# A decoder trunk whose SBUF pools are shifted by small free pieces

## The chip, the cores and the metric

One core of a Trainium2 chip runs the whole program. The metric is the device time of one execution in microseconds. Before the change it is 1892.44 us, the median of three runs (1891.72 to 1893.65 us).

## The reference

Two decoder layers on 256 tokens of 1024 channels, all in float32. Each layer first mixes tokens (three branches fed by one projection), then applies a feed-forward part: a dense SwiGLU in the first layer, two of eight SwiGLU experts per token in the second.

```python
for l in range(DEPTH):
    h = rms_norm(x) * (1 + sc1) + sh1
    x = x + g1 * token_mixer(h, ...)   # gated delta net, Mamba-2, latent attention, gates, w_out
    h = rms_norm(x) * (1 + sc2) + sh2
    if l % 2 == 0:
        f = swiglu(h, ffn_w_gate[i], ffn_w_up[i], ffn_w_down[i])      # 1024 -> 2816 -> 1024
    else:
        f = moe_ffn(h, router, w_gate, w_up, w_down)                  # 8 experts, 1024 -> 3584 -> 1024
    x = x + g2 * f
return rms_norm(x, final_norm_w)
```

## The kernel before, in words

Every large product is made from two halves of each operand, high and low (float32r): `mm3` (line 98) issues three matmuls, high by high, high by low and low by high, through the helper `mm` (line 95, whose instruction stands at line 96). The first operand of `mm` is stationary, the second is streamed; the profile names a matmul as output<-streamed,stationary.

Weights come in pieces of 1 MB (128 partitions x 2048 columns) by DMAs on SyncE's queue into `raw` buffers of 8 KB per partition, requested ahead. `chunk` (line 160) splits a piece: ScalarE copies 1024 columns into a high half `whi` (line 170), VectorE subtracts it for the low half `wlo` (line 172). The halves lie in a ring (line 151): four buffers of 4 KB of each kind and, in the expert stage, for every fifth one more in another pool. TensorE's use of a buffer is what gives it back to ScalarE, and the low half's reading of a raw buffer is what lets the next load start.

The stages in order:

- `mixer` of layer 0 and 1 (line 533). Its projections stream either the weights with the activations `hh`/`hl` stationary (`tok_gemm`, `tmajor_gemms`), 512 columns wide, or, in `conv` (line 563), the activations with the weights stationary, 256 columns wide. Branch projections have `yh`/`yl` stationary. The output projection (`tmajor_gemms`, line 430, called at the end of `mixer`) takes its first column half out of the ring and its second out of 2 KB tiles `ohi`/`olo` in the mixer's own pool (`wg`, line 539).
- `dense_ffn` (line 1222) with `hh`/`hl`, then `ah`/`al` stationary.
- `moe` (line 1310): eight times `expert` (line 1551), each for up to 128 tokens that `gather` (line 1507) picked by a product with a selection matrix `Pm` into `xx`. Gate and up: seven groups of 512 hidden columns, in each 48 matmuls that stream the ring with `xx` stationary, then `inner` (line 1558: SiLU, product, four transposes, split into `act`). Down: 168 matmuls that stream the ring with `act` stationary. `outer` (line 1589) scales the result and adds it to the tokens by a product with `PTm`; it runs beside the next expert's first groups. The order of ScalarE's and VectorE's instructions around the splits is fixed by `behind`, which queues an instruction after a named one on its engine.

SBUF is laid out by pools, from the left end upward and, for pools with side="right", from the right end downward; within a pool tiles follow each other in the order of their first use, in steps of 32 bytes. Where the operands start, modulo 256 bytes, by the program's list of tiles:

| tiles | start in bytes | modulo 256 |
| --- | --- | --- |
| `raw`, `whi`, `wlo` (pool wp) | 35296, 59872, 76256 | 224 |
| `hh`, `hl` (and `h2` in their place later) | 92640, 100832 | 224 |
| `act`, `tg`, `ah`/`al`, `yh`/`yl` of the mixer, other tiles of the right side | right side ends at 229344 | 224 |
| the mixer's 2 KB tiles (`ohi`, `olo` and others) | from 113760 | 96 |
| `Pm` | 109312 | 0 |
| `xx`, `sg`, `PTm` of the experts | 117856, 134240, 140384 | 96 |
| `yh` of the experts' output | 142656 | 64 |
| `xs`, `cst` | 17024, 25216 | 128 |

Pieces inside a tile that a matmul reads begin at multiples of 512 bytes from the tile's start, but for the 336-column pieces of the small projection.

Of the kernel before, what the change touches and what calls it, by code (L numbers as in the profile page):

```python
# [10 lines left out]
F32 = mybir.dt.float32  # L11
# [8 lines left out]
P = 128  # L20
# [41 lines left out]
def trunk_kernel(ctx, tc, a, out, dbg=None):  # L62
# [4 lines left out]
    cp = ctx.enter_context(tc.tile_pool(name="cp", bufs=1))  # L67
    wp = ctx.enter_context(tc.tile_pool(name="wp", bufs=2))
    pp = ctx.enter_context(tc.tile_pool(name="pp", bufs=2, space=PSUM))

    ones = cp.tile([P, P], F32, name="ones")
    V.memset(ones, 1.0)
    xs = cp.tile([P, NT, D], F32, name="xs")
# [1 line left out]
    pv = [cp.tile([P, NPP], F32, name=f"pv{l}") for l in range(DEPTH)]  # L75
    pos = cp.tile([P, NT], I32, name="pos")
    rt = cp.tile([P, KD, NE], F32, name="rt")
    ident = cst[:, C_ID:C_ID + P]
    U = cst[:, C_U:C_U + P]
    mask = cst[:, C_MASK:C_MASK + P]  # L80
# [64 lines left out]
    def load_raw(src, k, n, raw=None):  # L145

        raw = raw_tile() if raw is None else raw
        last["load"] = nc.sync.dma_start(raw[:, :k * n], src)
        return raw
# [38 lines left out]
    def sstile():  # L188
        return pp.tile([P, 512], F32, name="sst", tag="ss", bufs=1)
# [343 lines left out]
    def mixer(l, after=None):  # L533

        with tc.tile_pool(name=f"mx{l}", bufs=1, reuse_waits="tile") as mp, \
                tc.tile_pool(name=f"mb{l}", bufs=1, reuse_waits="tile", side="right") as bp, \
                tc.tile_pool(name=f"mc{l}", bufs=1, reuse_waits="tile", side="right") as qp:

            def wg(name, dt=F32):
                return mp.tile([P, 512], dt, name=name, tag="w2k", bufs=16)  # L540
# [766 lines left out]
    def shot(pool, i, name, dt=F32):  # L1307
        return pool.tile([P, 2048], dt, name=name, tag=f"shot{i}")

    def moe(l):  # L1310
        with tc.tile_pool(name=f"mw{l}", bufs=1, reuse_waits="tile", side="right") as xp, \
                tc.tile_pool(name=f"mo{l}", bufs=1, reuse_waits="tile") as mp:
            for i in range(6):
                xp.tile([P, 2048], F32, name="raw", tag=f"rx{i}")

            extra.update(order=[(xp, f"rx{i}", 1) for i in (3, 4)] + [own] * 2 + [(xp, f"rx{i}", 1) for i in (2, 0, 1, 5)] + [own])
            turn[0] = 0
            ahead.extend(load_raw(w, 4, 512, shot(xp, i, "raw")) for i, w in enumerate(first_srcs[3:7]))
            ahead.extend(load_raw(w, 4, 512) for w in first_srcs[7:15])
            h2 = [mp.tile([P, NT, D], F32R, name="h2", tag="h2", bufs=2) for _ in range(2)]  # L1320
            slot = mp.tile([P, NT, NE], F32, name="slot")
            wsel = mp.tile([P, NT, NE], F32, name="wsel")
            sel = mp.tile([P, NT, NE], F32, name="sel")
            ovi = mp.tile([P, 4], I32, name="ovi")
            ovs = mp.tile([P, 3, 2, NT], F32, name="ovs")
            with tc.tile_pool(name=f"mr{l}", bufs=1, reuse_waits="tile") as rp, \
                    tc.tile_pool(name=f"me{l}", bufs=1, reuse_waits="tile") as ep:
                rest, weights = route(l, rp, h2, slot, wsel, sel)
                pair = lambda e: choose(mp, [lambda t, i=i: slot[:, t, i:i + 1] for i in (e, e + 1)])
                Pm = pair(0)  # L1330
                behind("Pm", rest)
                ready = [(x, Pm, i) for i, x in enumerate(gather(l, ep, h2, Pm, 2, True))]
                behind("xl", weights)
                late = {16: 2, 17: 3, 27: 3}
                ahead.extend(load_raw(first_srcs[i], 4, 512, shot(xp, late[i], "raw") if i in late else None)
                             for i in range(15, 28))
                row_tile[l, 5] = lambda: mp.tile([P, 512], F32, name="g2", tag="g2", bufs=2)
                ada_rows(l, 5)
                g2 = [rows[l, 10 + c] for c in range(2)]

                def after_first(c):
                    if c == 1:
                        with tc.issue_after(last["act"].ins), tc.issue_after(last["tr"].ins):
                            overflow_data(ep, slot, wsel, sel, ovi, ovs)
                def finish():

                    fw, o, f = (raw_tile() for _ in range(3))
                    nc.sync.dma_start(fw[:, :D], a["final_w"])
                    o, f = (x.rearrange("p (t n) -> p t n", t=NT) for x in (o, f))
                    for t in range(NT):  # L1350
                        rs = rms_scale(t, lambda c: o[:, t, c * 512:(c + 1) * 512])
                        for c in range(2):
                            cs = slice(c * 512, (c + 1) * 512)
                            G.tensor_mul(f[:, t, cs], xs[:, t, cs], fw[:, cs])
                        for c in range(2):
                            cs = slice(c * 512, (c + 1) * 512)
                            if c:
                                V.tensor_scalar(o[:, t, cs], f[:, t, cs], rs, None, op0=OP.mult)
                            else:
                                A.activation(o[:, t, cs], f[:, t, cs], AF.Copy, scale=rs)  # L1360
                            nc.sync.dma_start(out[t * P:(t + 1) * P, cs], o[:, t, cs])

                for e in range(NE):
                    x, Pm, i = ready.pop(0)

                    def between():
                        Pm = behind("lo", pair, e + 1)
                        ready.extend((x, Pm, i) for i, x in enumerate(gather(l, ep, h2, Pm, 2)))
                    expert(l, e, ep, xp, x, lambda t, Pm=Pm, i=i: Pm[:, t, i], lambda t, e=e: wsel[:, t, e:e + 1], g2,
                           after_first if e == 0 else None, between if e % 2 and e < NE - 1 else None)  # L1370
                stages.flush()
                finish()
                overflow(l, mp, ep, xp, h2, g2, ovi, ovs, finish)
            extra.clear()

# [93 lines left out]
    def overflow_data(rp, slot, wsel, sel, ovi, ovs):  # L1469


        iota = cst[:, C_IOTA:C_IOTA + P]
        ps = sstile()
        mm(ps[:, :NE], ones, sel[:, 0], True, False)
        mm(ps[:, :NE], ones, sel[:, 1], False, True)
        over = rp.tile([P, NE], F32, name="over")
        V.tensor_scalar(over, ps[:, :NE], float(P), None, op0=OP.is_gt)
        rank = rp.tile([P, NE], F32, name="rank")
        G.memset(rank[:, 0:1], 0.0)
        for e in range(1, NE):  # L1480
            G.tensor_add(rank[:, e:e + 1], rank[:, e - 1:e], over[:, e - 1:e])
        ovf = rp.tile([P, 4], F32, name="ovf")
        V.tensor_reduce(ovf[:, 0:1], over, axis=AX.X, op=OP.add)
        tmp8 = rp.tile([P, NE], F32, name="tmp8", tag="tmp8", bufs=2)
        for r in range(3):
            ohr = rp.tile([P, NE], F32, name="ohr", tag="ohr", bufs=2)
            V.scalar_tensor_tensor(ohr, rank, float(r), over, op0=OP.is_equal, op1=OP.mult)
            V.tensor_mul(tmp8, ohr, iota[:, :NE])
            V.tensor_reduce(ovf[:, r + 1:r + 2], tmp8, axis=AX.X, op=OP.add)
            for t in range(NT):  # L1490
                V.tensor_mul(tmp8, ohr, slot[:, t])
                V.tensor_reduce(ovs[:, r, 0, t:t + 1], tmp8, axis=AX.X, op=OP.add)
                V.tensor_mul(tmp8, ohr, wsel[:, t])
                V.tensor_reduce(ovs[:, r, 1, t:t + 1], tmp8, axis=AX.X, op=OP.add)
            V.tensor_scalar(ovs[:, r, 0], ovs[:, r, 0], -float(P), None, op0=OP.add)
        V.tensor_copy(ovi, ovf)

    def choose(mp, slots):

        Pm = mp.tile([P, NT, 2, P], F32R, name="Pm", tag="Pm", bufs=2)  # L1500
        for i, slot in enumerate(slots):
            for t in range(NT):
                last["Pm"] = V.tensor_scalar(Pm[:, t, i], cst[:, C_IOTA + 1:C_IOTA + P + 1], slot(t), None,
                                             op0=OP.is_equal)
        return Pm
# [40 lines left out]
    def behind(name, trace, *args, **kw):  # L1546

        with tc.issue_after(last[name].ins):
            return trace(*args, **kw)  # L1549
# [129 lines left out]
    def ffn_hidden(tile, done=False):  # L1679
# [4 lines left out]
        make_hT(tile, 0, 3, 4, tiles=[0])  # L1684
        ffn_scale["newton"] = last["newton"]
    lead = {}
    tgpool = tc.tile_pool(name="tg", bufs=1, reuse_waits="tile", side="right")
    tgp = tgpool.__enter__()
    mixer(0, ffn_hidden)
# [35 lines left out]
    if stop <= 3:  # L1725
        return
    moe(1)


# [66 lines left out]
```

## Time and profile before

| | |
| --- | --- |
| median of three runs | 1892.44 us (1891.72 to 1893.65) |
| the profiled execution | 1891.01 us, of which its span is 1889.2 us |
| mean granted TensorE clock | 0.996 of full speed |
| busy: TensorE, its weight loads | 1841.5 us (97%), 1545.4 us (82%) |
| busy: VectorE, ScalarE, GpSimd | 1602.2 us (85%), 1231.6 us (65%), 43.3 us (2%) |
| read from HBM | 527.41 MB, 280 GB/s over the span |

Busy times of an engine are the union of its instructions' spans. A matmul's span includes its way through the array and overlaps the next one's, so TensorE's rate is read from the starts of successive matmuls. The expert stage is the span's part from some 866 us on; its eight experts take 84 to 85 us each for gate and up and 38.6 or 44.2 us for down.

### The profile page before, as it was taken

How to read it: one execution, taken by the hardware profiler on the slowest of the kernel's cores; microseconds unless marked ns; L12 is line 12 of the kernel's file. 1: busy time of each engine (PE TensorE's matmuls, PEld its weight loads, DVE VectorE, ACT ScalarE, POOL GpSimd, SP SyncE). 2: the span in 40 equal slices, each digit the busy share in tenths (PEclk: the TensorE clock that was granted, in tenths of full speed). 3: DMA queues.
4: the chain of work that ended last, by engine and by line, in shares of the span. 5: the costliest groups of instructions: out<-in, count | busy, mean ns of one | idle time of the engine just before them, and what ended most of it. 6: DMA issues, size and time to landing. Idle time of an engine off the chain costs nothing.

```text
span 1889.2 us, 25651 instructions
## 1 busy us (share of the span) xinstructions
PE 1841.5 (97%) x9490; PEld 1545.4 (82%) x9490; DVE 1602.2 (85%) x2313; ACT 1231.6 (65%) x1599; POOL 43.3 (2%) x61
## 2 busy tenths in 40 slices
PE   8999999999999999999999999999999999999996
PEld 6899887788889998888887878878778888788785
DVE  7998788777578978877999989998898999899997
ACT  4665445644466644457777777777877777777775
POOL 0000010000000000100000000000000000000001
PEclk9999999999999999999999999999999999999998
DMA  9453457677644654758998989999899999899892
GB/s 365 160 202 131 171 198 270 235 257 263 211 144 148 221 184 173 276 204 357 340 354 331 356 313 362 363 359 349 331 352 344 354 363 367 307 357 378 336 353 84
DMA packets 75016, 530.19 MB, mean 281 GB/s; under 512 B 8578, under 2 KB 8962, under 8 KB 12548
## 3 DMA queue, kind: packets, MB, share of 16 engines
q1 hardware_dynamic: 74884, 528.49, 74.1%
q8 instruction: 76, 1.25, 0.3%
q14 instruction: 56, 0.46, 0.1%
HBM read 527.41 MB, written 1.05 MB: 280 GB/s over the span
## 4 chain that ended last, share of the span: by engine, by line
PE 87%; DVE 6%; ACT 3%; issue 2%; DMA 2%; DVEq 0%; ACTq 0%; SPq 0%
PE mmt L96 76%; PE smt L96 6%; DVE wlo L172 2%; PE sst L96 2%; PE trt L1566 1%; DVE raw L199 1%; ACT whi L170 1%; PE trt L258 1%; ACT sg L1527 1%; DMA raw<-in_ffn_w_down_dram 0%; PE trt L1073 0%; PE trt L96 0%; DMA raw<-in_w_ada_pair_dram 0%; DMA raw<-in_w_out_dram 0%; DMA raw<-in_w_ada_gate_dram 0%
## 5 line engine op out<-in xcount | busy, mean ns | idle before, releaser
L172 DVE TENSOR_TENSOR wlo<-raw,whi 128x1024 fp32r<-128x1024 f32 (+1 forms) x874 | 1043.7, 1223 | 128.1 <-ACT whi L170 107.1
L170 ACT ACTIVATE whi<-raw 128x1024 fp32r<-128x1024 f32 (+1 forms) x874 | 908.2, 1059 | 305.2 <-PE mmt L96 253.4
L96 PE MATMUL mmt<-whi,xx 128*128 128x512 f32 x1792 | 579.0, 398 | 0.0
L96 PEld LDWEIGHTS mmt<-whi,xx 128*128 128x128 f32 x1792 | 337.4, 188 | 75.0
L96 PE MATMUL mmt<-wlo,xx 128*128 128x512 f32 x896 | 357.6, 399 | 4.9 <-DVE wlo L172 4.9
L96 PE MATMUL mmt<-whi,act 128*128 128x512 f32 x896 | 281.0, 391 | 1.2 <-ACT whi L170 1.2
L96 PEld LDWEIGHTS mmt<-wlo,xx 128*128 128x128 f32 x896 | 168.8, 188 | 52.3 <-DVE wlo L172 16.4
L96 PEld LDWEIGHTS mmt<-whi,act 128*128 128x128 f32 x896 | 167.5, 188 | 36.4 <-ACT whi L170 2.5
L96 PE MATMUL mmt<-whi,hh 128*128 128x512 f32 (+2 forms) x480 | 184.0, 389 | 5.8 <-ACT hh L292 2.0
L96 PE MATMUL mmt<-whi,hl 128*128 128x512 f32 (+2 forms) x480 | 181.1, 383 | 0.5 <-DVE hl L293 0.5
L96 PE MATMUL mmt<-wlo,hh 128*128 128x512 f32 (+2 forms) x480 | 181.2, 383 | 0.0
L96 PE MATMUL mmt<-wlo,act 128*128 128x512 f32 x448 | 175.3, 391 | 1.8 <-DVE wlo L172 1.6
L199 DVE CUSTOM_DVE_ANT_0 raw<-raw,sc_b,pv 128x1024 f32<-128x1024 f32 x96 | 123.2, 1298 | 12.8 <-DMA raw<-in_w_ada_pair_dram 9.8
L96 PEld LDWEIGHTS mmt<-whi,hh 128*128 128x128 f32 x480 | 91.0, 190 | 23.7 <-ACT hh L292 2.6
L96 PEld LDWEIGHTS mmt<-whi,hl 128*128 128x128 f32 x480 | 90.7, 189 | 18.0 <-DVE hl L293 1.0
L96 PEld LDWEIGHTS mmt<-wlo,hh 128*128 128x128 f32 x480 | 90.9, 189 | 16.2 <-DVE wlo L172 0.2
L96 PEld LDWEIGHTS mmt<-wlo,act 128*128 128x128 f32 x448 | 84.1, 188 | 22.3 <-DVE wlo L172 4.4
L96 PE MATMUL mmt<-hh,whi 128*128 128x256 f32 x320 | 92.3, 290 | 0.5 <-ACT whi L170 0.5
L96 PE MATMUL mmt<-hh,wlo 128*128 128x256 f32 x320 | 90.6, 287 | 1.1 <-DVE wlo L172 1.1
L96 PE MATMUL mmt<-hl,whi 128*128 128x256 f32 x320 | 91.0, 285 | 0.0
L1549 ACT ACTIVATE act<-trt 128x512 fp32r<-128x512 f32 x56 | 33.1, 591 | 72.0 <-PE trt L1566 72.0
L1549 DVE TENSOR_TENSOR act<-trt,act 128x512 fp32r<-128x512 f32 x56 | 38.6, 689 | 33.2 <-ACT act L1549 32.7
(422 smaller groups left out, 2226.9 us busy)
## 6 DMA issues: line engine op xcount, KB each, us to landing
raw<-in_moe_w_gate_dram SPq DMA_DIRECT2D x112, 1024.0 KB, 6.0
raw<-in_moe_w_up_dram SPq DMA_DIRECT2D x112, 1024.0 KB, 6.2
raw<-in_moe_w_down_dram SPq DMA_DIRECT2D x112, 1024.0 KB, 6.9
raw<-in_w_in_dram SPq DMA_DIRECT2D x50, 1024.0 KB, 4.9
raw<-in_w_ada_pair_dram SPq DMA_DIRECT2D x32, 1024.0 KB, 5.0
raw<-in_w_ada_gate_dram SPq DMA_DIRECT2D x16, 1024.0 KB, 4.9
raw<-in_ffn_w_down_dram SPq DMA_DIRECT2D x11, 1024.0 KB, 5.5
raw<-in_ffn_w_gate_dram SPq DMA_DIRECT2D x10, 1024.0 KB, 4.9
```

The lines of the kernel that those rows point to most:

```text
L96: return T.matmul(o, l, r, start=start, stop=stop, skip_group_check=True)
L170: last["hi"] = A.activation(hi[:, :m], r, AF.Copy)
L172: last["lo"] = V.tensor_sub(lo[:, :m], r, hi[:, :m].bitcast(F32))
L199: last["ada"] = V.tensor_tensor_reduce(r, r, sc_b, 1.0, pv[l][:, PP_BADA + i:PP_BADA + i + 1], OP.mult, OP.add, modc[l][:, i:i + 1])
L258: T.transpose(ps[:, j * S + t * P:j * S + (t + 1) * P], src(t, b0 + j), ident)
L1527: A.activation(tmp[:, o], ps[:, o], AF.Identity, scale=sc, bias=sh)
L1549: return trace(*args, **kw)
L1566: last["tr"] = T.transpose(ps[:, b * P:(b + 1) * P], sg[:, b * P:(b + 1) * P], ident)
```

## The change

Six tiles that nothing writes or reads are allocated so that what follows them in their pools moves: 32 bytes in the constants' pool, 128 at the head of the mixer's pool, 224 in the expert stage's pool, 160 and 32 in its inner pool, and a pool of 224 bytes at the right end ahead of all others of that side. No instruction is added or removed.

```diff
+    def gap(pool, n):
+
+        pool.tile([P, n // 4], F32, name="gap", tag=f"gap{n}")
+
...
     rt = cp.tile([P, KD, NE], F32, name="rt")
+    gap(cp, 32)
...
                 tc.tile_pool(name=f"mc{l}", bufs=1, reuse_waits="tile", side="right") as qp:
+
+            gap(mp, 128)
...
             ovs = mp.tile([P, 3, 2, NT], F32, name="ovs")
+            gap(mp, 224)
             with tc.tile_pool(name=f"mr{l}", bufs=1, reuse_waits="tile") as rp, \
                     tc.tile_pool(name=f"me{l}", bufs=1, reuse_waits="tile") as ep:
+                gap(ep, 160)
...
                             overflow_data(ep, slot, wsel, sel, ovi, ovs)
+                            gap(ep, 32)
...
     lead = {}
+    edge = ctx.enter_context(tc.tile_pool(name="edge", bufs=1, side="right"))
+    gap(edge, 224)
     tgpool = tc.tile_pool(name="tg", bufs=1, reuse_waits="tile", side="right")
```

The starts that follow: the ring 59872+32 = 59904, the raw buffers 35328 and `hh` 92672, all multiples of 256; the mixer's 2 KB tiles 113760+32+128 = 113920; `xx` 117856+32+224+160 = 118272; the experts' `yh` 142656+448 = 143104; the right side ends at 229344-224 = 229120. `Pm` goes to 109568 and stays at a multiple of 256; `xs` and `cst` don't move.

## Rows read from the trace of the kernel before

**Rows 1.** The page: busy time and share of TensorE; the chain by engine.

```profile
PE 1841.5 (97%) x9490; PEld 1545.4 (82%) x9490; DVE 1602.2 (85%) x2313; ACT 1231.6 (65%) x1599; POOL 43.3 (2%) x61
...
PE 87%; DVE 6%; ACT 3%; issue 2%; DMA 2%; DVEq 0%; ACTq 0%; SPq 0%
```

**Rows 2.** Stretches of one expert: length, busy us per engine (instructions), clock, DMA.

```profile
1381.00:1393.00 12.00, 11.22 (x50) 8.89 (x50) 12.00 (x14) 8.05 (x9) 0.00 (x0) 1.00 0.82 311
1405.00:1454.50 49.50, 49.50 (x221) 39.63 (x220) 44.15 (x42) 37.98 (x42) 0.00 (x0) 1.00 0.93 348
1454.50:1493.20 38.70, 38.70 (x174) 31.95 (x173) 35.52 (x32) 29.98 (x30) 0.00 (x0) 1.00 0.98 387
```

**Rows 3.** Waits from 900 to 1860 us: total us, times, longest.

```profile
ACT whi L170 <- PE mmt L96: 126.1, 380, 2.7
...
PEld mmt L96 <- DVE wlo L172: 20.9, 44, 1.1
```

**Rows 4.** Timeline of TensorE, gate/up: start us, length us, then the instructions.

```profile
1405.13 0.39 PE L96 MATMUL mmt<-wlo,xx 128*128 128x512 f32 x1
...
1412.80 0.39 PE L96 MATMUL mmt<-wlo,xx 128*128 128x512 f32 x1
```

**Rows 5.** The same timeline, down projection of the last expert.

```profile
1854.05 0.39 PE L96 MATMUL mmt<-wlo,act 128*128 128x512 f32 x1
...
1869.01 0.39 PE L96 MATMUL mmt<-wlo,act 128*128 128x512 f32 x1
```

**Rows 6.** The same timeline, output projection of layer 0.

```profile
320.08 0.39 PE L96 MATMUL mmt<-whi,hl 128*128 128x512 f32 x1
...
322.12 0.39 PE L96 MATMUL mmt<-whi,hl 128*128 128x512 f32 x1
...
322.58 0.39 PE L96 MATMUL mmt<-ohi,hh 128*128 128x512 f32 x1
...
326.54 0.40 PE L96 MATMUL mmt<-ohi,hl 128*128 128x512 f32 x1
```

**Rows 7.** The same timeline, conv of layer 0 and a gather of the experts.

```profile
112.39 0.28 PE L96 MATMUL mmt<-hl,whi 128*128 128x256 f32 x1
...
114.78 0.28 PE L96 MATMUL mmt<-hh,whi 128*128 128x256 f32 x1
...
1608.57 3.90 PE L96 MATMUL trt<-Pm,h 128*128 128x256 f32 x32
```

**Rows 8.** TensorE's groups by shape: xcount | busy us, mean ns | idle us before.

```profile
L96 PE MATMUL mmt<-whi,xx 128*128 128x512 f32 x1792 | 579.0, 398 | 0.0
L96 PE MATMUL mmt<-wlo,xx 128*128 128x512 f32 x896 | 357.6, 399 | 4.9 <-DVE wlo L172 4.9
L96 PE MATMUL mmt<-whi,act 128*128 128x512 f32 x896 | 281.0, 391 | 1.2 <-ACT whi L170 1.2
L96 PE MATMUL mmt<-wlo,act 128*128 128x512 f32 x448 | 175.3, 391 | 1.8 <-DVE wlo L172 1.6
L96 PE MATMUL mmt<-whi,hh 128*128 128x512 f32 x424 | 169.0, 399 | 2.0 <-ACT hh L1196 2.0
...
L96 PE MATMUL mmt<-hh,whi 128*128 128x256 f32 x320 | 92.3, 290 | 0.5 <-ACT whi L170 0.5
...
L96 PE MATMUL mmt<-whi,yh 128*128 128x512 f32 x96 | 38.1, 397 | 0.0
```

**Rows 9.** Timeline of VectorE, one group of gate/up.

```profile
1045.25 7.01 DVE L172 TENSOR_TENSOR wlo<-raw,whi 128x1024 fp32r<-128x1024 f32 x6 [0.26 <-ACT whi L170]
1052.18 0.68 DVE L1549 TENSOR_TENSOR sg<-sg,mmt 128x512 f32<-128x512 f32 x1
```

**Rows 10.** Timeline of TensorE, output of one expert.

```profile
1375.46 0.39 PE L96 MATMUL smt<-yh,PTm 128*128 128x512 f32 x1
...
1376.39 0.40 PE L96 MATMUL smt<-yh,PTm 128*128 128x512 f32 x1
```

## The prediction

> **What bounds the kernel now.** The page comes first: TensorE is busy for 97% of the span, and the chain that ended last is 87% TensorE [rows 1]. A stage view says whether anything else is as full: in the expert stage, over half of the span, the granted clock is 1.00 (the upper level, 2.4 GHz), TensorE is busy throughout but for 0.8 us of the stretch from 1381 us, and VectorE is close behind (44.15 of 49.50 us, but 12.00 of 12.00 us there, where an expert's output overlaps the next one's first groups) [rows 2]. The waits of that stage agree: ScalarE waits 126 us for TensorE to give weight buffers back, TensorE waits only some 21 us for VectorE's low halves, and no engine of the list waits for a load [rows 3]. So what counts is how fast TensorE takes one matmul after another, and a change that issues nothing new can only act there, or through other engines' access to the moved tiles.
>
> A matmul's duration (some 0.39 us) overlaps its neighbours', so I read start to start from the timeline, over stretches without a wait. Gate/up: 1405.13 to 1412.80 us, 33 matmuls (each row shown is every third), 232.4 ns each [rows 4]. Down: 1854.05 to 1869.01 us, 66 matmuls, 226.7 ns [rows 5]. Both are 512 columns wide and stream the same ring buffers; the stationary operand differs: xx starts at 96 modulo 256 bytes, act at 224, like the ring. The output projection gives the same pair with the roles exchanged: the stationary operand hh (224) stays, the moving one is the ring (224) from 320.08 to 322.12 us, 9 matmuls, 226.7 ns; then ohi/olo (96) from 322.58 to 326.54 us, 17 matmuls, 232.9 ns [rows 6]. Two stages, either operand: 96 in place of 224 costs about 6 ns. One kind already has its moving operand at 0: the 256-column gather out of Pm, 32 matmuls in 3.90 us, (3.90-0.28)/31 = 116.8 ns; the conv matmuls, 256 columns with both at 224, take (114.78-112.39)/20 = 119.5 ns [rows 7]. So 0 is better than 224 by 2.7 ns for the moving side.
>
> **The change, part by part.** No instruction, transfer or wait is added or removed: a gap tile is never written or read, so nothing queues on it, on SP or POOL or anywhere. That costs nothing because there is nothing to hide.
>
> *The 32 bytes behind cp* move the ring, the raw buffers and hh/hl from 224 to 0; *edge* moves everything on the right side (act, ah/al, tg, yh, lh) from 224 to 0; *the mx gap* moves the 2 KB mixer tiles (ohi/olo) from 96 to 0; *the gaps in mp and ep* move xx, sg, PTm from 96 and the output's yh from 64 to 0. Every wide matmul of the four classes below then has both operands at 0.
>
> What both at 0 cost, no row shows. From above: no better than both at 224, 226.7 ns. From below: the moving side's 2.7 ns, and for the stationary side as much as 96 against 224 is worth, 5.7 ns [rows 4, 5]: 226.7-2.7-5.7 = 218.3 ns. I take 2.7 ns for each side, 221.3 ns, because the gather is the only row at 0, and because scaling the 512-column 226.7 ns by 116.8/119.5 also gives 221.6.
>
> The sum, counts from the grouped view [rows 8]:
> - gate/up, 1792+896 = 2688 matmuls, 232.4 to 221.3: 29.8 us;
> - down, 896+448 = 1344, 226.7 to 221.3: 7.3 us;
> - projections of mixer and dense FFN and the branches, 3x424+3x96 = 1560, 226.7 to 221.3: 8.4 us;
> - conv, 3x320 = 960 of 256 columns, 2.7 ns (the stationary side is left out, a 256-column matmul leaves less time to load it): 2.6 us.
>
> That is 48.1 us on TensorE. Not all arrives. In the expert stage VectorE makes a low half every 7.01/6 = 1.17 us [rows 9], eight per group of 512 hidden columns, and two 512-column steps at some 0.6: 10.6 us, while TensorE's group takes 48 x 232.4 ns = 11.2 us and four transposes now, and 10.6 us and the transposes after. So VectorE still just keeps up, except in the two first of an expert's seven groups, where it is full [rows 2]: a faster TensorE reaches the end of the ring there and waits for the low halves. I strike two sevenths of the gate/up term: 21.3 us left. Of the down term I keep 5.5 us (every second expert gathers the next rows there, with VectorE's work in it). Of the other 11.0 us I keep six tenths, 6.6 us: mixers have chains on VectorE and ScalarE between their matmuls. Together 33.4 us.
>
> The profiled execution took 1891.0 us (span 1889.2 us and 1.8 us around it), 1.4 us under the median of 1892.4 us. 1891.0-33.4 = 1857.6 us; on the median 1859.0 us.
>
> *Loads, ScalarE, VectorE* I cost at nothing. All these tiles shift together, so two operands of one vector instruction keep their distance, and the loads end no wait in the expert stage [rows 3]. If the cover went, VectorE would show it first: one per cent more on its low half is 0.012 us x 8 per group, a tenth of a us, no more than the transposes still leave.
>
> **The rivals.**
>
> *Only evened out.* 0 is no better than 224, and what is gained is that xx and ohi lose their disadvantage: 5.7 ns x 2688 = 15.3 us, five sevenths of it 10.9 us: 1881.5 us. For it: the gather differs from the conv in more than its place (other tiles, another stage). Against: the 2.7 ns are there in the only stretch with an operand at 0.
>
> *More than forecast.* The stationary side gains its full 5.7 ns: 218.3 ns. 14.1 ns x 2688 x 5/7 = 27.1 us, 8.4 ns x 1344 = 11.3 us of which 8.5, and 8.4 ns x 1560 + 2.6 us at six tenths, 9.4 us: 45.0 us, 1847.4 us. For it: xx against act is the larger of the two differences that the rows show and is on that side. Against: a group is then 48 x 218.3 ns = 10.5 us and the transposes against VectorE's 10.6 us, so this is about where VectorE takes over. The Trainium skill (TensorE: Matmul & The Clock Gate, "Wait — 56ns, not 53.3ns?") gives 215.7 ns from start to start at 512 columns and full clock; the rows here stand 11 to 17 ns above it, and by that figure the same sum would come to an estimated 59 us.
>
> *No change.* The cadence belongs to something other than the start address: which pool, how the loops alternate PSUM tiles (down alternates two, gate/up fills one), or what VectorE does beside it; or the layout doesn't come out as meant. Then 1892.4 us. Against: the output projection's two runs lie next to each other in one loop with the same hh and differ by 6.2 ns [rows 6]. The Trainium skill says as much for this rival (SBUF — State Buffer, "Specifications (TRN2)"): SBUF lines are of 16 bytes, and by that 96, 224 and 0 would be alike; its section "Operand start alignment" asks for multiples of the element size only, and says that this is about legality, not speed. The trace does not agree, with 226.7 against 232.9 ns.
>
> *Slower: 224 is the good place and 0 is not.* Two operands that start alike are not fast for that alone: sg and PTm, both at 96, and yh (64) with PTm run at (1376.39-1375.46)/4 = 232.5 ns [rows 10]. If 0 is like 96, the down, projection and branch matmuls go from 226.7 to 232.5 ns: 5.8 ns x 2904 = 16.8 us, nearly all on the path because VectorE is not in its way: 1907 us. It decides once both at 0 cost more than the mean of today, (2688x232.4+2904x226.7)/5592 = 229.4 ns. Against: the gather again.
>
> **How the numbers follow.** Forecast 0.50, evened out 0.17, more 0.18, no change 0.08, slower 0.07. The time is the forecast's, 1859 us. Range: the two outer cases and some us for how much arrives (all of the 48.1 us would give 1844 us; more than that only with the lower bound of the cadence): 1837 to 1884 us, leaving out the last two cases. The forecast's own range is 1850 to 1869 us. Faster by over 0.2% (3.8 us, about what a measurement of this kernel can tell from no change) are the first three cases, 0.85; within 0.2% 0.08; slower 0.07.
>
> **What would show it.** In the profile after: the same counts per group; the timeline's gate/up and down stretches without waits at one cadence, near 221 ns; ohi/olo no slower than the ring; conv near 117 ns; TensorE's waits for VectorE's low halves up from some 21 us, at the start of each expert; VectorE's low half still 1223 ns in the mean. The forecast is wrong if gate/up comes down to 226.7 ns and down stays (evened out), if neither moves, or if down rises.

## The result: 0.59% faster, less than a third of the forecast gain

The changed kernel takes 1882.36 us, the median of five runs (1878.96 to 1882.70), against 1892.44 us for the kernel before, five runs too (1891.72 to 1897.14). The ratio is 0.9941 [0.9928, 0.9954]: 10.1 us gained where 33.4 were forecast. The direction holds, and so does the range; the size is the one of *only evened out*, 1881.5 us.

The profiled execution took 1880.15 us, its span 1878.4 us. From the page: busy time and share of each engine, to stand beside [rows 1].

```profile
PE 1829.8 (97%) x9490; PEld 1543.9 (82%) x9490; DVE 1601.1 (85%) x2313; ACT 1231.8 (66%) x1599; POOL 42.0 (2%) x61
```

The counts are those of before. TensorE is busy for 11.7 us less, its weight loads for 1.5 us less, and no other engine's time moved by more than 1.3 us. TensorE's groups by shape (xcount | busy us, mean ns | idle before) say which matmuls it was:

```profile
L101 PE MATMUL mmt<-whi,xx 128*128 128x512 f32 x1792 | 571.7, 394 | 0.0
L101 PE MATMUL mmt<-wlo,xx 128*128 128x512 f32 x896 | 353.9, 395 | 4.8 <-DVE wlo L177 4.7
L101 PE MATMUL mmt<-whi,act 128*128 128x512 f32 x896 | 281.1, 391 | 0.9 <-ACT whi L175 0.9
```

Only the two groups with `xx` differ from [rows 8]: 579.0 to 571.7 and 357.6 to 353.9 us. The others of [rows 8], down with `act` shown here among them, repeat their numbers within 0.2 us, although all their operands moved from 224 to 0.

The cadence, which is the time from one matmul's start to the next one's, from the timeline of TensorE (start us, length us, instructions). First gate/up, ten periods of three matmuls; then the four transposes that end a group and the low halves that follow:

```profile
1411.26 0.39 PE L101 MATMUL mmt<-wlo,xx 128*128 128x512 f32 x1
...
1418.06 0.39 PE L101 MATMUL mmt<-wlo,xx 128*128 128x512 f32 x1
...
1418.52 0.60 PE L1577 MATMUL trt<-cst,sg 128*128 128x128 f32 x4
...
1419.19 0.40 PE L101 MATMUL mmt<-wlo,xx 128*128 128x512 f32 x1
...
1421.28 0.39 PE L101 MATMUL mmt<-wlo,xx 128*128 128x512 f32 x1
```

(1418.06-1411.26)/30 = 226.7 ns, where [rows 4] had 232.4. Right behind the transposes it is slower: (1421.28-1419.19)/9 = 232.2 ns. From the same view, down (66 matmuls in [rows 5]; here 84):

```profile
1837.97 0.39 PE L101 MATMUL mmt<-wlo,act 128*128 128x512 f32 x1
...
1857.01 0.39 PE L101 MATMUL mmt<-wlo,act 128*128 128x512 f32 x1
```

And the output projection's `ohi`/`olo`:

```profile
323.72 0.39 PE L101 MATMUL mmt<-ohi,hl 128*128 128x512 f32 x1
...
327.80 0.39 PE L101 MATMUL mmt<-ohi,hl 128*128 128x512 f32 x1
```

Down: 19.04 us for 84 matmuls, 226.7 ns, as before. `ohi`/`olo`: 18 in 4.08 us, 226.7 ns, down from 232.9 [rows 6]. The 256-column kinds, conv and gather:

```profile
112.43 0.28 PE L101 MATMUL mmt<-hh,whi 128*128 128x256 f32 x1
...
114.58 0.28 PE L101 MATMUL mmt<-hh,whi 128*128 128x256 f32 x1
...
1600.56 4.00 PE L101 MATMUL trt<-Pm,h 128*128 128x256 f32 x32
```

Conv: 18 in 2.15 us, 119.4 ns, unchanged. The gather went the other way: (4.00-0.28)/31 = 120.0 ns, up from 116.8 [rows 7]. Its streamed `Pm` stays at 0; what moved is `h2`, from 224 to 0.

Where the time went, by stage, from the starts of the first matmuls of each phase in the two traces:

| stretch | before, us | after, us | gained |
| --- | --- | --- | --- |
| to the first gate matmul | 865.8 | 866.1 | -0.3 |
| gate/up, eight phases | 677.9 | 667.0 | 10.9 |
| down, the first seven phases | 287.1 | 287.2 | 0.0 |

The spans differ by 10.8 us: all of it is gate/up. The first row isn't a clean zero, though. TensorE's granted clock fell to 0.50 (1.2 GHz) for a few us of layer 0's output projection in the trace after, and not in the trace before. In both TensorE had waited 1.48 us for `hh` just ahead of this. The windows before and after (length, then busy us of TensorE, its weight loads, VectorE, ScalarE and GpSimd, the granted clock, DMA share, GB/s):

```profile
316.40:318.20 1.80, 1.80 (x11) 1.52 (x10) 1.80 (x5) 0.17 (x2) 0.00 (x0) 1.00 0.29 36
316.40:318.20 1.80, 1.80 (x6) 1.37 (x5) 1.80 (x5) 0.52 (x2) 0.00 (x0) 0.50 0.24 50
```

From 310 to 325 us the clock is 1.00 in the mean before and 0.89 after. Over 15 us that is some 1.7 us at most, so a gain of that size ahead of the experts would not show in it.

### The profile page after: what moved, and what is told of

It reads as the page before. It is cut to its first block, busy times and chain, and to the rows that moved or that the text cites. A ratio compares the mean times of both kernels' runs of the same rounds, so it can differ in the third digit from the quotient of the medians.

```text
span 1878.4 us, 25651 instructions
## 1 busy us (share of the span) xinstructions
PE 1829.8 (97%) x9490; PEld 1543.9 (82%) x9490; DVE 1601.1 (85%) x2313; ACT 1231.8 (66%) x1599; POOL 42.0 (2%) x61
## 4 chain that ended last, share of the span: by engine, by line
PE 86%; DVE 7%; ACT 4%; issue 2%; DMA 1%; DVEq 0%; ACTq 0%; SPq 0%
PE mmt L101 75%; PE smt L101 6%; DVE wlo L177 2%; DVE raw L204 1%; PE sst L101 1%; PE trt L1577 1%; ACT whi L175 1%; PE trt L263 1%; ACT sg L1538 1%; DMA raw<-in_w_in_dram 1%; PE trt L1080 0%; PE trt L101 0%; ACT whi L352 0%; DMA raw<-in_w_out_dram 0%; DMA raw<-in_w_ada_pair_dram 0%
## 5 line engine op out<-in xcount | busy, mean ns | idle before, releaser
L177 DVE TENSOR_TENSOR wlo<-raw,whi 128x1024 fp32r<-128x1024 f32 (+1 forms) x874 | 1042.6, 1224 | 124.2 <-ACT whi L175 100.7
L101 PE MATMUL mmt<-whi,xx 128*128 128x512 f32 x1792 | 571.7, 394 | 0.0
L101 PE MATMUL mmt<-wlo,xx 128*128 128x512 f32 x896 | 353.9, 395 | 4.8 <-DVE wlo L177 4.7
L1560 DVE TENSOR_TENSOR act<-trt,act 128x512 fp32r<-128x512 f32 x56 | 38.6, 689 | 28.6 <-ACT act L1560 28.2
```

Source lines behind the costliest of these rows:

```text
L101: return T.matmul(o, l, r, start=start, stop=stop, skip_group_check=True)
L177: last["lo"] = V.tensor_sub(lo[:, :m], r, hi[:, :m].bitcast(F32))
```

## The experiments

The theory after the result: one address alone is neither good nor bad. What counts is how far apart TensorE's two operands start, modulo 256 bytes. The first rival is that 96 is a bad start for the stationary operand (or 0 a good one); the second, that another engine's or a DMA's access to the moved tiles is what differs. Diffs are against the changed kernel unless said otherwise; in a diff, "..." stands for lines left out.

**A scan of `xx`.** The ring stays at 0, `xx` of expert e starts at 32 x e bytes. The gaps ahead of it are changed to suit.

```diff
...
-        xx = ep.tile([P, 2, 2, KD, P], F32R, name="xx", tag="xx")
+        room = ep.tile([P, 4096 + 64], F32R, name="xx", tag="xx")
+        o = 16 * nth[0]
+        nth[0] = (nth[0] + 1) % 4
+        xx = room[:, o:o + 4112].rearrange("p (e r) -> p e r", e=2)[:, :, :2048].rearrange("p e (i k n) -> p e i k n", i=2, k=KD)
```

> The experts' stationary tile begins 32 bytes further for each expert: expert 0 at 0 modulo 256, expert 1 at 32, up to expert 7 at 224; the ring (moving) stays at 0. Read per expert: start to start of gate/up matmuls away from waits. Theory distance (what counts is how far the two operands of a matmul lie apart modulo 256): 226.7 ns at expert 0, 232 to 233 at expert 4 (128 apart, as xx and the ring were before), something of its own at each other expert, and at 224 perhaps under 226.7, since the 256-column gather was faster with its moving operand 32 bytes above its stationary one. Theory place (some starts are good by themselves, 0 and 224 among them): 226.7 ns at experts 0 and 7, 232 to 233 at experts 1 to 6. Theory that neither counts: all alike. Time: 1882 to 1892 us, not the point.

One run: 1888.05 us (the kernel before, measured beside it, 1891.23). The timeline of TensorE, 33 matmuls of gate/up in each pair, for experts 0 (0 bytes), 2 (64) and 6 (192):

```profile
886.39 0.39 PE L101 MATMUL mmt<-wlo,xx 128*128 128x512 f32 x1
...
893.87 0.39 PE L101 MATMUL mmt<-wlo,xx 128*128 128x512 f32 x1
...
1137.56 0.39 PE L101 MATMUL mmt<-wlo,xx 128*128 128x512 f32 x1
...
1145.26 0.40 PE L101 MATMUL mmt<-wlo,xx 128*128 128x512 f32 x1
...
1643.79 0.39 PE L101 MATMUL mmt<-wlo,xx 128*128 128x512 f32 x1
...
1651.34 0.39 PE L101 MATMUL mmt<-wlo,xx 128*128 128x512 f32 x1
```

226.7, 233.3 and 228.8 ns. In the order 0, 32, ... 224 the eight are 226.7, 233, 233, 234, 232, 233, 229, 233. So it is no slope and no special 96: everything off 0 costs 5 to 7 ns, but for 192 with some 2. 224, at which both operands ran at 226.7 ns before, costs 233.2 when the ring is at 0. That already speaks for the distance.

**Everything moved by 64.** No operand at a multiple of 256, all distances kept.

```diff
-    gap(cp, 32)
+    gap(cp, 96)
...
-    gap(edge, 224)
+    gap(edge, 160)
```

> The changed kernel with every tile moved by the same 64 bytes: ring, hh, xx, act, ohi, Pm all at 64 modulo 256, none of them at a multiple of 256. Theory distance: nothing changes, 1882 us, 226.7 ns at 512 and 119.5 ns at 256 columns. Theory place: 64 is none of the good starts, 232 ns for all 512-column matmuls, and the time 1900 us or more (5.5 ns x 5600 matmuls = 31 us on TensorE, half of it or more on the path).

1879.33 us (1876.87 to 1880.83), 0.9934 [0.9917, 0.9950] of before; 226.7 ns in gate/up of every expert. The multiple of 256 does nothing by itself.

**Only `xx`, `sg` and `PTm` apart.** They stand 128 bytes from the ring; all else as changed.

```diff
-                gap(ep, 160)
+                gap(ep, 32)
...
-                            gap(ep, 32)
+                            gap(ep, 160)
```

> The changed kernel with the gap in the experts' inner pool 32 in place of 160 bytes, so that xx, sg and PTm are back at 128 bytes from the ring, all else as in the changed kernel. Theory distance and theory place alike: gate/up back at 232.4 ns, and nearly the whole gain given back, 1891 us; the projections keep theirs. If the gain came from somewhere else than the experts' gate/up: near 1882 us.

1891.52 us (1888.14 to 1892.88), 0.9996 [0.9986, 1.0005] of before: the whole gain is gone. Gate/up of every expert is at 232.1 to 232.5 ns, 33 matmuls each, read as in the scan.

So the gaps of the constants, the mixer and the right side together bring nothing that can be measured.

**One gap alone.** The kernel before, with 128 bytes in the expert stage's inner pool, so that `xx` starts at 224 like the ring. Against the kernel before:

```diff
+    def gap(pool, n):
+
+        pool.tile([P, n // 4], F32, name="gap", tag=f"gap{n}")
...
+                gap(ep, 128)
```

> The kernel before with one gap only, 128 bytes in the experts' inner pool: xx, sg and PTm at 224 like the ring, nothing at a multiple of 256. Theory distance: gate/up at 226.7 ns and nearly the whole gain, 1882 to 1883 us. Theory that a start at a multiple of 256 counts: 1892 us.

1881.27 us (1880.35 to 1883.38), 0.9952 [0.9935, 0.9968] of before. Gate/up has both operands at 224:

```profile
1387.32 0.39 PE L100 MATMUL mmt<-wlo,xx 128*128 128x512 f32 x1
...
1394.80 0.39 PE L100 MATMUL mmt<-wlo,xx 128*128 128x512 f32 x1
```

33 matmuls in 7.48 us, 226.7 ns. One gap of six does what the six do.

**Finer steps.** Ring at 0; the experts' `xx` at 256, 264, -8, 0, 4, 12, 16 and 24 bytes from it, modulo 512.

```diff
...
+        room = ep.tile([P, 4096 + 104], F32R, name="xx", tag="xx")
+        o = [32, 94, 97, 100][nth[0]]
```

> As the first scan, in small steps: the experts' stationary tile begins 256, 264, -8, 0, 4, 12, 16 and 24 bytes from the ring modulo 512 (experts 0 to 7). Theory distance modulo 256: expert 0 like expert 3, at 226.7 ns; of the others no row tells yet. If the reads meet in pieces of 32 bytes or more, -8 is bad and 4 to 24 are like 0 or like 32 (233 ns); if there is a distance better than 0, it shows as a cadence under 226 ns. If the period is 512, expert 0 is at 232 to 233 ns.

One run, 1892.46 us (the kernel before, measured beside it, 1890.72). Expert 4, at 4 bytes, 33 matmuls:

```profile
1396.39 0.39 PE L101 MATMUL mmt<-wlo,xx 128*128 128x512 f32 x1
...
1404.06 0.40 PE L101 MATMUL mmt<-wlo,xx 128*128 128x512 f32 x1
```

232.4 ns, where expert 3 at 0 bytes has 226.7: four bytes are enough to lose it. 256 is as good as 0 (226.7); 264 gives 230.7, -8 233.3, and 24 230 to 231. At 12 and 16 bytes there is no one pace. Expert 6, at 16, in two stretches:

```profile
1662.44 0.40 PE L101 MATMUL mmt<-wlo,xx 128*128 128x512 f32 x1
...
1668.04 0.40 PE L101 MATMUL mmt<-wlo,xx 128*128 128x512 f32 x1
...
1685.12 0.39 PE L101 MATMUL mmt<-wlo,xx 128*128 128x512 f32 x1
...
1691.24 0.39 PE L101 MATMUL mmt<-wlo,xx 128*128 128x512 f32 x1
```

24 matmuls in 5.60 us are 233.3 ns each, 27 in 6.12 us 226.7 ns. Expert 5, at 12, changes between 226.7, 230.0 and 233.3 ns in the same way. So in the runs so far gate/up is fast at every equal start modulo 256, while off it the distance alone does not always fix the pace.

**TensorE alone.** Behind the last output of the changed kernel stand blocks of 24 matmuls on one tile `h`, with nothing else running: 512 or 256 columns, the stationary operand d floats behind the streamed one, which starts at m.

```diff
...
+        for j, (n, m, d) in enumerate(jobs):
+            ps = (mmtile if j % 2 else smtile)()
+            for _ in range(24):
+                mm(ps[:, :n], x[:, 1024 + d:1024 + d + P], x[:, m:m + n], True, True)
```

> The changed kernel with 41 blocks of 24 matmuls appended behind the last output, when VectorE, ScalarE and the loads are idle; one float32r tile gives both operands, the stationary one 0 to 512 bytes (in steps down to 4) further than the moving one modulo 256, 512 columns and 256 columns wide, also with both starts moved together and with only the moving one moved. Theory distance between TensorE's own two reads: the same numbers as in the stages, 226.7 ns at 0 and 232 to 234 ns at 32, 96 and 128 bytes, also without other engines, and both moved together like 0. Theory that other engines' reads and writes meet TensorE's: with them idle all distances give one cadence, nearer to 216 ns. Time: some 250 us longer, not the point.

One row of the timeline is one block; of 512 columns at distances of 64, 128, 252, 256 and 512 bytes, with both operands moved by 64, and with both moved by 20:

```profile
1911.57 5.75 PE L101 MATMUL smt<-h 128*128 128x512 f32 x24
...
1933.94 5.76 PE L101 MATMUL smt<-h 128*128 128x512 f32 x24
...
1978.53 5.61 PE L101 MATMUL smt<-h 128*128 128x512 f32 x24
1983.97 5.62 PE L101 MATMUL mmt<-h 128*128 128x512 f32 x24
1989.43 5.60 PE L101 MATMUL smt<-h 128*128 128x512 f32 x24
1994.87 5.64 PE L101 MATMUL mmt<-h 128*128 128x512 f32 x24
...
2005.85 5.80 PE L101 MATMUL mmt<-h 128*128 128x512 f32 x24
```

A window over some of them, with the columns of the windows above:

```profile
1967.00:1989.00 22.00, 22.00 (x98) 18.04 (x97) 0.00 (x0) 0.00 (x0) 0.00 (x0) 1.00 0.00 1
```

A block is 23 intervals and one matmul of 0.39 us: 233.0, 233.5, 227.0, 227.4, 226.5, 228.3 and 235.2 ns. With VectorE, ScalarE and GpSimd at 0.00 us and no load to speak of the difference is all there, so it lies within TensorE's own reads, and the second rival falls. Two blocks are limits to the theory. Equal starts that are off by 20 bytes are as slow as unequal ones, and 252 bytes, which is 4 below an equal start, are as fast as 256.

**Only the right side apart.** `act` (and `ah`/`al`, `yh`) 128 bytes from the ring, all else as changed.

```diff
-    gap(edge, 224)
+    gap(edge, 96)
```

> The changed kernel with 96 in place of 224 bytes at the right end: act, ah/al, yh and the rest of that side begin 128 bytes from the ring, experts' gate/up as in the changed kernel. Theory distance: down 232.4 ns, 5.7 ns x 1344 = 7.7 us on TensorE, the branch and dense-FFN down products 5.7 ns x 528 = 3.0 us, and the conv no different: 1889 to 1893 us against 1882 us. Theory that only the experts' gate/up (xx) is sensitive: 1882 us.

1888.53 us (1885.27 to 1890.58), 0.9984 [0.9974, 0.9993] of before. Down of the last expert, 128 matmuls in 29.74 us, 232.3 ns:

```profile
1833.89 0.39 PE L101 MATMUL mmt<-wlo,act 128*128 128x512 f32 x1
...
1863.63 0.40 PE L101 MATMUL mmt<-wlo,act 128*128 128x512 f32 x1
```

The down phases go from 38.6 and 44.3 us to 39.5 and 45.0 in turn; over eight experts that is 4 x 0.9 + 4 x 0.7 = 6.4 us. The kernel before, measured beside it, took 1890.72 us, so 2.2 us are left of a gain of 10.1. The products with `ah`/`al` and `yh`/`yl` slowed to some 232 ns as well, but ahead of the experts no loss shows: the first gate matmul starts at 864.4 us here and at 866.1 in the changed kernel. That leaves the time just under the 1889 to 1893 us expected. The fast cadence of down, which the kernel before had already, was a matter of distance too.

**A few bytes below.** The same kind of blocks, to see whether a buffer can stand a little below the ring, keep 512 columns fast as stationary operand, and make 256 columns faster as streamed one.

```diff
+        lower = [64, 63, 62, 61, 60, 59, 58, 56, 54, 52, 48]
+        jobs = [(n, m, d) for s in lower for n, m, d in ((512, 64, s), (256, s, 64))] * 2
```

> The changed kernel with 44 blocks of 24 matmuls behind its last output, all other engines idle (22 places, each twice): 512 columns with the stationary operand at the moving one's place or 4, 8, 12, 16, 20, 24, 32, 40, 48, 64 bytes below it, and 256 columns with the moving operand so much below the stationary one. It asks whether a buffer can stand a few bytes below the ring and keep 512-column matmuls (as stationary operand) at the fast cadence while 256-column matmuls (as moving operand) become faster. If the fast 512-column places of the first such run (227 ns at 0, 4 and 16 bytes below) are a property of the distance, 0, 4 and 16 bytes give 226 to 228 ns again in both passes and most others 230 to 234 ns. If they were chance of single blocks, the two passes differ from each other by more than 2 ns. For 256 columns: 119.5 ns at 0, 115 to 118 ns at some of 4 to 24 bytes by the first run; if that was chance, 119 to 120 ns everywhere. The time of the whole program says nothing here: it has the blocks added.

Second pass: 512 columns at 0, 256 at 0, 512 at -4, 512 at -16, 256 at 20 bytes:

```profile
1956.76 5.60 PE L101 MATMUL smt<-h 128*128 128x512 f32 x24
1962.20 3.03 PE L101 MATMUL mmt<-h 128*128 128x256 f32 x24
1965.07 5.77 PE L101 MATMUL smt<-h 128*128 128x512 f32 x24
...
1990.46 5.65 PE L101 MATMUL smt<-h 128*128 128x512 f32 x24
...
2004.32 2.94 PE L101 MATMUL mmt<-h 128*128 128x256 f32 x24
```

226.5, (3.03-0.28)/23 = 119.6, 233.9, 228.7 and 115.7 ns. The places whose blocks ran undivided in both passes repeat within 0.5 ns, but one: 512 columns at -4 took 226.7 in the first pass (and in "TensorE alone"), 233.6 by the single starts in the second. It has two states, as 16 bytes had in the finer steps, and the distance does not choose between them. For 256 columns the equal start is not the good one at all: 115.7 ns at 20 bytes, 117.1 at 16, 119.6 at 0. There too the distance is not enough: the stationary operand 64 bytes behind the streamed one took (2.89-0.28)/23 = 113.5 ns in the blocks of "TensorE alone",

```profile
2039.49 2.89 PE L101 MATMUL mmt<-h 128*128 128x256 f32 x24
```

and (2.99-0.28)/23 = 117.8 ns in these, from other starts:

```profile
2046.34 2.99 PE L101 MATMUL mmt<-h 128*128 128x256 f32 x24
```

No place keeps both: at -16 the projections would lose 2 ns and conv gain 2.5. A layout with conv's gain, 960 x 2.5 ns = 2.4 us (some 6 us if 113.5 ns were to be had there) less what the projections lose, was not built. No version that was run beats the changed kernel by more than can be measured.

**Start-up.** Gate/up was at 226.7 ns only from about the tenth matmul behind a group's transposes. Blocks of 30 at distance 0 (in one kind 256), with transposes, four short matmuls, a pause or nothing ahead; in some the stationary operand changes its 512 bytes with every matmul.

```diff
...
+            if "tr" in kind and kind != "pause":
+                pt = trtile()
+                for b in range(4):
+                    T.transpose(pt[:, b * P:(b + 1) * P], xf[:, 1024 + b * P:1024 + (b + 1) * P], ident)
...
+            for k in range(30):
+                b = (k % 3) * P if "three" in kind else 0
+                mm(ps, x[:, 1024 + d + b:1024 + d + b + P], x[:, 512:1024], True, True)
```

> The changed kernel with 24 blocks of 30 matmuls of 512 columns behind its last output, all other engines idle. Both operands start at a multiple of 256 bytes; before a block stands nothing, four transposes as in the expert stage, four matmuls of 128 columns, or one copy on VectorE for which TensorE must wait; in two kinds the stationary operand changes its 512 bytes with each matmul. One kind has the stationary operand 256 bytes on behind the transposes. It asks why the changed kernel's gate/up is at 226.7 ns only from about the tenth matmul after its four transposes or a wait, and at 230 to 232 ns before. If that start-up lies in TensorE's own stream: the first nine after transposes take 229 to 233 ns each here too, the blocks with nothing before them 226.7 ns from the first. If it is VectorE's or ScalarE's work beside them, or weights that arrive late: 226.7 ns from the first matmul in every block, since nothing runs beside them here. The time of the whole program says nothing: it has the blocks added.

The timeline; transposes of one block were put ahead of another, so a block is read by what stands before it here:

```profile
1900.08 6.96 PE L101 MATMUL smt<-h 128*128 128x512 f32 x30
1906.88 0.60 PE L1680 MATMUL trt<-cst,h 128*128 128x128 f32 x4
1907.23 7.10 PE L101 MATMUL mmt<-h 128*128 128x512 f32 x30
```

6.96 us is 29 intervals of 226.6 ns and 0.39 us, from the first matmul on. Behind transposes it is 7.10 us. The starts of the single matmuls of that block are 316, 235, 233, 236, 224, 231, 236, 228, 233 and 230 ns apart, and from there on 226 or 227. So the start-up is TensorE's own. It was not separated from a pause: the blocks with VectorE's copy ahead had transposes there too. Transposes are not needed for it, though: in "TensorE alone" the block moved by 64 bytes, right behind a block at 226.7 ns, has its first ten starts 225 to 236 ns apart and is at 226.7 from there on.

## Why the prediction was right or wrong

**The step that failed** is "0 is better than 224 by 2.7 ns for the moving side", and with it "I take 2.7 ns for each side, 221.3 ns". The gather and the conv of [rows 7] differ in two ways that bear on the step: the streamed operand's start (0 and 224), and the distance of the two (32 bytes and 0). The step put the 2.7 ns down to the first. The trace after keeps `Pm` at 0, takes the distance away, and the gather rises from 116.8 to 120.0 ns. The run of finer steps puts `Pm` at 32 and `h2` at 0, 32 bytes apart as before with the streamed operand off 0, and the gather is back at 116.8 ns:

```profile
1358.72 3.90 PE L101 MATMUL trt<-Pm,h 128*128 128x256 f32 x32
```

At 256 columns a distance can pay, as the blocks at 16 and 20 bytes show; at 512 columns it costs. A row of 256 columns was carried over to 512 by scaling, and that was the second fault of the same step. The figure 221.3 does not occur: no stretch at 512 columns in any run stood below 226.5 ns.

By terms, forecast to arrive against gained: gate/up 21.3 us, 10.9 measured; down 5.5 us, 0.0; projections, branches and conv 6.6 us, -0.3 (with up to 1.7 us of slower clock in it). No cadence that needed 0 to be better than 224 moved: down 226.7 ns, conv 119.4. The part that only needed 96 to lose its disadvantage came.

**The price of the disadvantage** was right: 5.7 ns from [rows 4, 5], 232.4 to 226.7 ns measured. So was the comparison of [rows 6], and `ohi`/`olo` lost their 6.2 ns, on too few matmuls to show.

**How much arrives** came out in gate/up at the share forecast, for another cause. Of that term five sevenths were kept, because VectorE was to hold TensorE up at the start of each expert. The waits of the expert stage, from 900 to 1849 us (total us, times, longest), against [rows 3]:

```profile
PEld mmt L101 <- DVE wlo L177: 21.2, 44, 1.1
```

TensorE waits 21.2 us for low halves, against 20.9: not more. What is missing sits in the start-up. Taken over the starts of all gate/up matmuls, 932 of the 2472 intervals without a wait are among the first nine behind transposes or a wait; they take 230.6 ns in the mean, the rest 226.8. (230.6-226.7) x 932 = 3.6 us. The intervals with a wait (over 242 ns, with no other matmul between) sum to 46.3 us, 45.0 before: 1.3 us. 2688 x (232.5-226.7) = 15.6 us, less 3.6 and 1.3: 10.7 us, and 10.9 were measured. The two sevenths struck were 4.4 us of the rival's 15.3; that they fit is chance.

**The rivals.** *Only evened out* is what happened, with 1881.5 us against 1882.36, though its ground was another: 0 and 224 are alike as long as both operands start there. It had 0.17, and the rows gave it more support than that. The argument against it was the gather alone, one kind of another width, while four stretches at 512 columns ([rows 4, 5, 6]) were open to a reading by distance: 0 at 226.7 ns twice, and 128 at 232.4 and 232.9. Only [rows 10] spoke against that reading.

*Slower* fell with the run at 64. What was brought up for it, that `sg`/`PTm` at 96 and 96 beside `yh` and `PTm` are slow [rows 10], is not explained by equal distance alone: `yh` stood 32 bytes from `PTm`, and `sg` at none. After the change all three are at 0, and a run of these is at (1370.89-1369.98)/4 = 227.5 ns. With the one gap in the kernel before, `sg` and `PTm` are both at 224 and `yh` at 192, and it is at (1371.03-1370.10)/4 = 232.5 ns. After the change:

```profile
1369.98 0.39 PE L101 MATMUL smt<-yh,PTm 128*128 128x512 f32 x1
...
1370.89 0.39 PE L101 MATMUL smt<-yh,PTm 128*128 128x512 f32 x1
```

With the one gap:

```profile
1370.10 0.40 PE L100 MATMUL smt<-yh,PTm 128*128 128x512 f32 x1
...
1371.03 0.40 PE L100 MATMUL smt<-yh,PTm 128*128 128x512 f32 x1
```

By the unrounded starts [rows 10], the changed kernel and the one gap are at 231.2, 226.7 and 232.5 ns. The two kinds alternate, so in [rows 10] and with the one gap every second matmul has an unequal pair. The equal pairs beside them are no faster at 224 than they were at 96; it is not the place. *No change* in the form "which pool or loop, not the address" fell with the scan, which changes the address alone. The Trainium skill was weighed there too: SBUF — State Buffer, "Specifications (TRN2)", gives lines of 16 bytes. By those, places 64 or 128 bytes apart would be alike, and the trace goes on disagreeing: 226.7 against 233.3 ns. The same page says in "Who interferes with whom" that TensorE has two independent read ports, one for streamed operands and one for weight loads. The blocks with all other engines idle do not agree with "independent" in effect: a matmul takes 227.4 or 233.5 ns with the two starts 256 or 128 bytes apart.

*More than forecast* rested on the same failed step. The 215.7 ns of the Trainium skill (TensorE: Matmul & The Clock Gate, "Wait — 56ns, not 53.3ns?") was not reached even by TensorE alone at a granted clock of 1.00 (2.4 GHz): 226.6 ns, float32r with a weight load for each matmul.

**Loads, ScalarE and VectorE at nothing** was right: VectorE's low half is 1224 ns in the mean (1223 before), and ScalarE's and VectorE's busy times moved by 0.2 and 1.1 us.

## What to carry to other kernels

Before a number is read off one pair of rows, list every way in which the two differ: here the start of one operand and the distance of two changed together, and the row taken was of another width. Where matmuls reload their stationary operand each time, lay the two operands out at the same place modulo 256 bytes: one gap in one pool did all that six gaps did, and whether the common start was 0, 64 or 224 made no difference (one at 20 bytes was slow). Expect less than cadence times count, since behind transposes or a wait some ten matmuls run at nearly the old pace.

## What the runs showed of the hardware

- Two operands of one matmul of 512 columns slow each other by where they start: 226.7 ns at a distance of 0 or 256 bytes, 229 to 234 at most others. At 4 bytes below an equal start, and at 12 and 16 above, the same distance gave 226.7 ns in some stretches and up to 233.6 in others. At the upper clock level, 2.4 GHz, 226.7 ns are 544 cycles and 233.3 ns are 560: 32 and 48 more than the columns. At 256 columns the order is another: 119.6 ns at 0, 115.7 at 20 bytes, 113.5 or 117.8 at 64.
- At the lower level (a granted clock of 0.50 from 316.40 to 318.20 us after the change) five starts of 512 columns with operands at distance 0 are 425 ns apart, (318.15-316.45)/4, which is the 512 columns at 1.2 GHz and nothing more:

```profile
316.45 0.63 PE L101 MATMUL mmt<-ohi,hl 128*128 128x512 f32 x1
...
318.15 0.47 PE L101 MATMUL mmt<-olo,hh 128*128 128x512 f32 x1
```

The clock stands in the second window of the section on the result.

- A stream of 512-column matmuls needs some ten of them behind four transposes to find its pace, 316 ns for the first and 224 to 236 for the next nine.
